# Feed-forward input with stationary weights, and rstd carried by rows and to the output

## The chip, the core and the metric

The kernel runs on one core of one Trainium2 chip. The core has five engines with queues of their own: TensorE (PE in the profile, its weight loads PEld), VectorE (DVE), ScalarE (ACT), GpSimd (POOL) and SyncE (SP, which here only starts transfers). TensorE multiplies a stationary operand of 128 x 128, loaded ahead, with a moving operand of up to 512 columns, and writes to PSUM; the other engines work on SBUF, and VectorE and ScalarE on PSUM too. The metric is the time of one execution on the device in microseconds (us).

## The reference: one decoder layer over 256 tokens

One sequence of 256 tokens with 1024 features goes through a mixer of two branches (block attention and a linear recurrence), cross-attention over 256 memory tokens, and a gated feed-forward block, all in float32. The change lies in the last block and the final norm:

```
hn = rmsnorm(h, norm_ffn_g)                 # h * rstd(h) * gain
gu = hn @ w_ffn_in                          # 1024 -> 2 x 2816
h  = h + (silu(gu[..., :2816]) * gu[..., 2816:]) @ w_ffn_out
return rmsnorm(h, final_norm_g)
```

Here rstd is one number for each token, 1 / sqrt(mean of squares + 1e-6).

## The kernel before: three products for one, and weight blocks in order

**Numbers in two parts.** Every float32 operand of the large products is split into a high part, which TensorE's fast 32-bit format holds exactly, and a low part, the rest. A product is then three: high by high, high by low, low by high. Weights arrive as raw float32 and are split in the kernel by `prep`: ScalarE writes the high part (line 193), VectorE and POOL share the low part (line 197). One block is 1 MB (128 x 2048), and a block's products are called a unit here. `ORDER` lists the blocks, `nxt` gives the next one and prepares two ahead; three buffers each hold high and low parts, two hold raw blocks.

**Two forms of product.** `t_part` (lines 237 to 239) keeps tokens stationary: 128 tokens by 128 features are loaded, and 512 columns of weights stream past, three times for the three products. The result has tokens on partitions. `gemm_f` (lines 252 and 253) keeps weights stationary: 128 features by 128 outputs are loaded, and all 256 tokens stream past. Where the weight's high part is stationary, the tokens' high and low parts go through in one matmul of 2 x 256 columns, into two halves of a PSUM bank; for the weight's low part there is a second matmul of 256 columns, the tokens' high part alone, added to the first half. The result has output units on partitions, and the two halves of the bank still have to be summed; `ev_sum` does that. Before, this form is used for the keys and queries of the cross-attention alone (tile `psf`), on M2 (memory tokens, buffer P0) and on H1 (tokens, buffer P1).

**The feed-forward block before.** H, the residual stream, has tokens on partitions. `turn_h2(t, c)` (lines 1061 to 1065) transposes a quarter of it (token half t, feature half c) on TensorE, multiplies with the gain on VectorE, and splits it into h2h on ScalarE and h2l on POOL. rstd is not applied here. Quarters are turned while the product before, `wo_part` into `pso`, still runs; the last quarter, (1, 1), after the first `ffn_in`. The inner 2816 units are worked in eleven rounds of 256. `ffn_in` forms gate and value side by side in a bank of 512 columns for each token half (tile `psi`, 24 matmuls a block, two blocks a round). `gate` applies rstd as a scale per partition, in Silu and in the product. Its result has tokens on partitions, and the output product needs inner units there, so `turn_hid` transposes it with four matmuls on TensorE (tile `hidT`, line 1096) and `split` makes its two parts. `ffn_out` adds the round into four accumulators (tile `acc`, `out_part`), one round behind. At the end `out_part` runs by hand-picked pieces, with the last `turn_hid` after the first of them; then `add_out`, the final norm's sums and the stores.

**What sets the order.** TensorE's instructions stand in the order of the program text. The order on the other engines comes from the framework's scheduler, except in stretches under `manual_schedule`, of which the final norm is one. An engine runs its queue in order, so an instruction that waits holds up what stands behind it. PSUM has eight banks: four in pool `mm` (products) and four in pool `sm` (small work, and `acc` in the end).

Of the kernel before, what the change touches and what calls it, by code (L numbers as in the profile page):

```python
# [71 lines left out]
def lay(ws):  # L72
    out = np.empty((len(ORDER), 128, 2048), np.float32)
    for i, u in enumerate(ORDER):
        if u[0] == "F":
            w = ws[u[1]][:, u[2]:u[2] + 256]
            out[i].reshape(128, 8, 256)[...] = w.reshape(8, 128, 256).transpose(1, 0, 2)
        elif u[0] == "T":
            w = ws[u[1]][u[3] * 512:(u[3] + 1) * 512, u[2]:u[2] + 512]
            if i < 3:  # L80
                n = PIECES[i]
                out[i].reshape(n, 128, 4 // n, 512)[...] = w.reshape(n, 4 // n, 128, 512).transpose(0, 2, 1, 3)
            else:
                out[i].reshape(128, 4, 512)[...] = w.reshape(4, 128, 512).transpose(1, 0, 2)
        elif u[0] == "I":
            o = out[i].reshape(128, 4, 512)
            for m in range(2):
                w = ws["w_ffn_in"][u[2] * 512:(u[2] + 1) * 512, m * FH + u[1] * 256:m * FH + (u[1] + 1) * 256]
                o[:, :, m * 256:(m + 1) * 256] = w.reshape(4, 128, 256).transpose(1, 0, 2)
        else:  # L90
            w = ws["w_ffn_out"][u[1] * 256:(u[1] + 1) * 256]
            out[i].reshape(128, 2, 1024)[...] = w.reshape(2, 128, 1024).transpose(1, 0, 2)
    return out
# [24 lines left out]
def build(tc, A, out):  # L118
    nc = tc.nc
    V, SC, G, PE, SY = nc.vector, nc.scalar, nc.gpsimd, nc.tensor, nc.sync  # L120
    with ExitStack() as ctx:
# [119 lines left out]
        def by_k(w, k):  # L241
            return tuple(t.rearrange("p (k c) -> p k c", k=k) for t in w)

        def gemm_f(X2, evict):
            w = by_k(nxt(), 8)
            for m in range(2):
                a = slice(m * 128, (m + 1) * 128)
                ps = mm.tile([128, 2, 256], F32, name="psf", tag="mm")  # L250
                for k in range(8):
                    PE.matmul(ps, w[0][:, k, a], X2[:, :, k], start=k == 0, stop=False)  # L252
                    PE.matmul(ps[:, 0], w[1][:, k, a], X2[:, 0, k], start=False, stop=k == 7)  # L253
# [708 lines left out]

        def ev_sum(dh, dl, c):
            def ev(m, ps):
                t, u = t2b("kx", (128, 256)), t2("ku", (128, 256))
                SC.activation(u, ps[:, 1], AF.Copy)
                V.tensor_tensor(t, ps[:, 0], u, op=ALU.add)
                d = 2 * c + m
                SC.activation(dh[:, d], t, AF.Copy)
                G.tensor_tensor(dl[:, d], t, dh[:, d].bitcast(F32), op=ALU.subtract)  # L970
            return ev
# [76 lines left out]
        at[0] += 4  # L1048
        gfin = big("B4", "gfin", (128, 1024))
        SY.dma_start(gfin, A["gfin"].to_broadcast([128, 1024]))  # L1050
        h2h = big("B1", "h2h", dt=F32R)
        h2l = big("B2", "h2l", dt=F32R)
        def wo_part(ps, t, c, kh):
            t_part(ps, wo[2 * c + kh], (oxh, oxl), t, kh)

# [21 lines left out]


        ring = ("B7", "B14", "B10", "B11", "B12", "B6")
        X2 = (h2h, h2l)  # L1080
        hid, acc, two, psi, hm = {}, {}, {}, {}, {}

        def gate(o, t):
            r, ps = two["r"][:, t:t + 1], psi.pop((o, t))
            g = t2("fg", (128, 256))
            SC.activation(g, ps[:, 0:256], AF.Silu, scale=r)  # L1086
            u = t2b("fu", (128, 256))
            V.scalar_tensor_tensor(u, ps[:, 256:512], r, g, op0=ALU.mult, op1=ALU.mult)  # L1088
            hm[o, t] = u

        def turn_hid(o):
            bk = mm.tile([128, 2, 256], F32, name="hidT", tag="mm")
            for t in range(2):
                u = hm.pop((o, t))
                for j in range(2):
                    PE.transpose(bk[:, j, t * 128:(t + 1) * 128], u[:, j * 128:(j + 1) * 128], ident)
            hd = big(ring[o % 6], "hid", (128, 2, 2, 256), F32R)
            split(bk, hd[:, 0], hd[:, 1])
            hid[o] = hd

        def ffn_in(o, kh, t, w):
            if kh == 0:
                psi[o, t] = mm.tile([128, 512], F32, name="psi", tag="mm")
            t_part(psi[o, t], w, X2, t, kh)

        def out_part(o, w, t, c, home=None, u=0, v=512):
            if home is None and (t, c) not in acc:
# [52 lines left out]

        def add_out(ps, t, u, w):
            d = H[:, t, u:w]
            V.tensor_tensor(d, ps, d, op=ALU.add)
# [89 lines left out]
```

## Time and profile before

| | |
|---|---|
| time, median of 3 runs (lowest to highest) | 625.71 us (625.56 to 626.14) |
| the profiled execution | 625.74 us |
| its span, first to last instruction | 623.8 us |
| TensorE busy in the span | 615.6 us, 99% |
| VectorE, ScalarE, POOL busy | 62%, 53%, 59% |
| mean granted clock of TensorE | 0.997 of full speed |
| feed-forward block, from the first `psi` matmul | 431.8 us to the end |

The page of the profile gives busy times by engine, the span in 40 slices, the chain of work that ended last, and groups of instructions by source line. The timeline gives single instructions with start and length. A matmul's record runs from its start to the end of its passage through the array, and the next one starts before that; lengths of stretches of TensorE are therefore taken from start to start. In rows of a tile, three numbers of nanoseconds are the shortest, the median and the longest.

### The profile page before, as it was taken

The numbers are of one execution on the slowest core, as the hardware profiler recorded it, in microseconds if no ns is written. First come the engines' busy times: TensorE is split into PE (matmuls) and PEld (weight loads), VectorE is DVE, ScalarE is ACT, GpSimd is POOL, SyncE is SP. The second block draws the span as 40 slices with busy tenths as digits, with TensorE's granted clock in tenths as the row PEclk, the third lists the DMA queues.
The fourth block names the chain that finished last, engine by engine and source line by source line (L and its number), as shares of the span: only waits on it lengthen the run. The fifth ranks groups of instructions, "written<-read, shape, count | busy, mean of one in ns | idle before, by whom it ended". The sixth has DMA issues, their size and how long they took to land.

```text
span 623.8 us, 8477 instructions
## 1 busy us (share of the span) xinstructions
PE 615.6 (99%) x3135; PEld 513.1 (82%) x3135; DVE 386.8 (62%) x671; ACT 332.5 (53%) x537; POOL 371.0 (59%) x296
## 2 busy tenths in 40 slices
PE   8999999999999999999999999999999999999995
PEld 7888888888877877778888889888888888888884
DVE  7566878979766875748856456754444444444433
ACT  7775555234376856727447556644543444434432
POOL 3887834556544464355867876656655665566553
PEclk9999999999999999999999999999999999999998
DMA  8755353344433333545455545453355555455511
GB/s 344 290 210 194 143 189 148 135 136 143 188 143 136 136 136 134 204 169 185 157 211 187 182 174 187 140 199 134 133 179 172 192 203 185 169 190 198 203 68 67
DMA packets 16888, 107.50 MB, mean 172 GB/s; under 512 B 2000, under 2 KB 2640, under 8 KB 4560
## 3 DMA queue, kind: packets, MB, share of 16 engines
q1 hardware_dynamic: 16128, 106.14, 46.6%
q10 hardware_dynamic: 720, 0.84, 0.4%
q8 instruction: 24, 0.39, 0.3%
q14 instruction: 16, 0.13, 0.1%
HBM read 105.92 MB, written 1.05 MB: 171 GB/s over the span
## 4 chain that ended last, share of the span: by engine, by line
PE 98%; DMA 1%; POOL 0%; DVE 0%; issue 0%; ACT 0%; POOLq 0%; DVEq 0%; ACTq 0%
PE pst L237 14%; PE pst L239 14%; PE pst L238 14%; PE psi L237 6%; PE psi L239 6%; PE psi L238 6%; PE psf L252 5%; PE acc L237 3%; PE acc L239 3%; PE acc L238 3%; PE psf L253 2%; PE lp L609 2%; PE psg L511 1%; PE pso L237 1%; PE pso L239 1%; PE pso L238 1%
## 5 line engine op out<-in xcount | busy, mean ns | idle before, releaser
L197 POOL TENSOR_TENSOR lo<-raw,hi 128x448 fp32r<-128x448 f32 x172 | 270.2, 1587 | 182.4 <-ACT hi L193 179.5
L193 ACT ACTIVATE hi<-raw 128x1024 fp32r<-128x1024 f32 (+1 forms) x194 | 196.2, 1037 | 167.4 <-PE pst L239 61.0
L197 DVE TENSOR_TENSOR lo<-raw,hi 128x576 fp32r<-128x576 f32 (+2 forms) x194 | 199.0, 1031 | 134.1 <-ACT hi L193 131.9
L237 PE MATMUL pst<-hi,Xh 128*128 128x512 f32 x256 | 103.2, 403 | 0.0
L239 PE MATMUL pst<-hi,Xl 128*128 128x512 f32 x256 | 100.0, 391 | 0.0
L238 PE MATMUL pst<-lo,Xh 128*128 128x512 f32 x256 | 99.9, 390 | 0.0
L237 PE MATMUL psi<-hi,h2h 128*128 128x512 f32 x176 | 69.7, 396 | 0.0
L239 PE MATMUL psi<-hi,h2l 128*128 128x512 f32 x176 | 68.7, 390 | 0.0
L238 PE MATMUL psi<-lo,h2h 128*128 128x512 f32 x176 | 68.6, 389 | 0.0
L239 PEld LDWEIGHTS pst<-hi,Xl 128*128 128x128 f32 x256 | 48.1, 188 | 10.3
L237 PEld LDWEIGHTS pst<-hi,Xh 128*128 128x128 f32 x256 | 48.1, 188 | 9.8 <-issue 0.7
L238 PEld LDWEIGHTS pst<-lo,Xh 128*128 128x128 f32 x256 | 48.2, 188 | 9.1
L239 PEld LDWEIGHTS psi<-hi,h2l 128*128 128x128 f32 x176 | 33.0, 188 | 7.1
L238 PEld LDWEIGHTS psi<-lo,h2h 128*128 128x128 f32 x176 | 33.1, 188 | 6.6
L237 PEld LDWEIGHTS psi<-hi,h2h 128*128 128x128 f32 x176 | 33.1, 188 | 6.5
L237 PE MATMUL acc<-hi,hid 128*128 128x512 f32 x86 | 33.6, 391 | 0.0
L239 PE MATMUL acc<-hi,hid 128*128 128x512 f32 x86 | 33.5, 390 | 0.0
L238 PE MATMUL acc<-lo,hid 128*128 128x512 f32 x86 | 33.5, 389 | 0.0
L1088 DVE SCALAR_TENSOR_TENSOR fu<-psi,r_h,fg 128x256 f32<-128x256 f32 x22 | 10.6, 484 | 26.0 <-ACT fg L1086 26.0
L1086 ACT ACTIVATE fg<-psi,r_h 128x256 f32<-128x256 f32 x22 | 10.4, 475 | 29.9 <-PE psi L239 29.9
L252 PE MATMUL psf<-H,hi 128*128 128x512 f32 x64 | 22.8, 400 | 0.0
L252 PE MATMUL psf<-M,hi 128*128 128x512 f32 x64 | 22.5, 396 | 0.0
(344 smaller groups left out, 1127.0 us busy)
## 6 DMA issues: line engine op xcount, KB each, us to landing
raw<-w SPq DMA_DIRECT2D x94, 1024.0 KB, 4.8
raw<-w SPq DMA_DIRECT2D x4, 512.0 KB, 6.3
raw<-w SPq DMA_DIRECT2D x4, 256.0 KB, 4.2
H<-xtok SPq DMA_DIRECT2D x1, 1024.0 KB, 9.5
mraw<-mT SPq DMA_DIRECT2D x1, 1024.0 KB, 4.9
xraw<-xT SPq DMA_DIRECT2D x1, 512.0 KB, 6.4
gfin<-gfin SPq DMA_DIRECT2D x1, 512.0 KB, 3.7
out<-H SPq DMA_DIRECT2D x2, 256.0 KB, 2.0
```

What stands on the lines that cost most here:

```text
L193: SC.activation(hi[:, a], raw[:, a], AF.Copy)
L197: eng.tensor_tensor(lo[:, b], raw[:, b], hi[:, b].bitcast(F32), op=ALU.subtract)
L237: PE.matmul(ps, xh, h, start=first, stop=False)
L238: PE.matmul(ps, xh, l, start=False, stop=False)
L239: PE.matmul(ps, xl, h, start=False, stop=last)
L252: PE.matmul(ps, w[0][:, k, a], X2[:, :, k], start=k == 0, stop=False)
L253: PE.matmul(ps[:, 0], w[1][:, k, a], X2[:, 0, k], start=False, stop=k == 7)
L511: PE.matmul(pss[c][t], z[:, k, t * 128:(t + 1) * 128], ws[c][0][:, k], start=z is Xh and k == 0, stop=False)
L609: PE.matmul(ps[:, j], KS[:, a0 + j], QQ[:, a0 + j], start=True, stop=True)
L1086: SC.activation(g, ps[:, 0:256], AF.Silu, scale=r)
L1088: V.scalar_tensor_tensor(u, ps[:, 256:512], r, g, op0=ALU.mult, op1=ALU.mult)
```

## The change

The input product of the feed-forward block takes the form of `gemm_f`. A block now holds all 1024 features of 128 gate and 128 value columns, in place of 512 features of 256 and 256. Each block gives one PSUM bank for the gate (m = 0) and one for the value (m = 1), with inner units on partitions, so `turn_hid` is gone. h2h and h2l become two halves of one tile H2 in buffer P0, so that both parts of all tokens stream in one matmul.

rstd now varies along columns. For the gate, `rows_of` spreads it over all partitions (two transposes and a copy), and VectorE multiplies with these rows ahead of Silu. For the value it is left out, and `add_out` multiplies with it when the accumulated output is added to H, since it is a factor of a whole token there. `halves` sums the two parts of a bank: ScalarE copies the one, VectorE adds the other. The high part of the result is written by ScalarE and the low part by POOL, by VectorE in the last round's second block.

At the start, two blocks are taken together and four banks are held: the first four of eight feature groups for all four banks, `turn_h2(1, 1)` after the first bank's share, then rstd and `rows_of`, then the second four.

```diff
 lay(), blocks "I":
-            o = out[i].reshape(128, 4, 512)
+            o = out[i].reshape(128, 8, 256)
             for m in range(2):
-                w = ws["w_ffn_in"][u[2] * 512:(u[2] + 1) * 512, m * FH + u[1] * 256:m * FH + (u[1] + 1) * 256]
-                o[:, :, m * 256:(m + 1) * 256] = w.reshape(4, 128, 256).transpose(1, 0, 2)
+                c = m * FH + u[1] * 256 + u[2] * 128
+                o[:, :, m * 128:(m + 1) * 128] = ws["w_ffn_in"][:, c:c + 128].reshape(8, 128, 128).transpose(1, 0, 2)
...
+        def f_part(ps, w, X2, m, ks):
+            a = slice(m * 128, (m + 1) * 128)
+            for k in ks:
+                PE.matmul(ps, w[0][:, k, a], X2[:, :, k], start=k == 0, stop=False)
+                PE.matmul(ps[:, 0], w[1][:, k, a], X2[:, 0, k], start=False, stop=k == 7)
+
+        def halves(dst, ps):
+            u = t2("ku", (128, 256))
+            SC.activation(u, ps[:, 1], AF.Copy)
+            V.tensor_tensor(dst, ps[:, 0], u, op=ALU.add)
...
-        h2h = big("B1", "h2h", dt=F32R)
-        h2l = big("B2", "h2l", dt=F32R)
+        H2 = big("P0", "H2", (128, 2, 8, 256), F32R)
+        h2h, h2l = H2[:, 0], H2[:, 1]
...
-        def gate(o, t):
-            r, ps = two["r"][:, t:t + 1], psi.pop((o, t))
-            g = t2("fg", (128, 256))
-            SC.activation(g, ps[:, 0:256], AF.Silu, scale=r)
+        def gate(o, kh, m, ps):
+            if m == 0:
+                g = gates[o, kh] = t2("fg", (128, 256))
+                halves(g, ps)
+                V.tensor_tensor(g, g, rows2, op=ALU.mult)
+                SC.activation(g, g, AF.Silu)
+                return
+            if kh == 0:
+                hid[o] = big(ring[o % 6], "hid", (128, 2, 2, 256), F32R)
+            hh, hl = hid[o][:, 0, kh], hid[o][:, 1, kh]
             u = t2b("fu", (128, 256))
-            V.scalar_tensor_tensor(u, ps[:, 256:512], r, g, op0=ALU.mult, op1=ALU.mult)
-            hm[o, t] = u
-
-        def turn_hid(o):
-            bk = mm.tile([128, 2, 256], F32, name="hidT", tag="mm")
-            for t in range(2):
-                u = hm.pop((o, t))
-                for j in range(2):
-                    PE.transpose(bk[:, j, t * 128:(t + 1) * 128], u[:, j * 128:(j + 1) * 128], ident)
-            hd = big(ring[o % 6], "hid", (128, 2, 2, 256), F32R)
-            split(bk, hd[:, 0], hd[:, 1])
-            hid[o] = hd
-
-        def ffn_in(o, kh, t, w):
-            if kh == 0:
-                psi[o, t] = mm.tile([128, 512], F32, name="psi", tag="mm")
-            t_part(psi[o, t], w, X2, t, kh)
+            halves(u, ps)
+            V.tensor_tensor(u, u, gates.pop((o, kh)), op=ALU.mult)
+            SC.activation(hh, u, AF.Copy)
+            (V if (o, kh) == (NF // 2 - 1, 1) else G).tensor_tensor(hl, u, hh.bitcast(F32), op=ALU.subtract)
...
+        ws = [by_k(nxt(), 8) for _ in range(2)]
+        psi = {(i, m): f_bank("psi") for i in range(2) for m in range(2)}
+        for i in range(2):
+            for m in range(2):
+                f_part(psi[i, m], ws[i], H2, m, range(4))
+                if (i, m) == (0, 0):
+                    turn_h2(1, 1)
+        r_2 = rstd2(ssq2, "h2")
+        rows2 = rows_of(r_2, "h2", "rowsB")
+        for i in range(2):
+            for m in range(2):
+                f_part(psi[i, m], ws[i], H2, m, range(4, 8))
+                gate(0, i, m, psi[i, m])
...
-            w = by_k(nxt(), 4)
-            for t in range(2):
-                ffn_in(o, kh, t, w)
-                if (o, kh, t) == (0, 0, 0):
-                    turn_h2(1, 1)
-                    two["r"] = rstd2(ssq2, "h2")
-                if kh == 1:
-                    gate(o, t)
-            if kh == 0 and o:
-                turn_hid(o - 1)
+            w = by_k(nxt(), 8)
+            for m in range(2):
+                ps = f_bank("psi")
+                f_part(ps, w, H2, m, range(8))
+                gate(o, kh, m, ps)
...
         out_part(n - 1, wa, 0, 0)
-        turn_hid(n)
         out_part(n - 1, wa, 0, 1)
...
         def add_out(ps, t, u, w):
             d = H[:, t, u:w]
-            V.tensor_tensor(d, ps, d, op=ALU.add)
+            V.scalar_tensor_tensor(d, ps, r_2[:, t:t + 1], d, op0=ALU.mult, op1=ALU.add)
```

More of the change, by code (lines that the diff above doesn't have):

```diff
@@ L242, in by_k, with f_bank @@
             return tuple(t.rearrange("p (k c) -> p k c", k=k) for t in w)
+        def f_part(ps, w, X2, m, ks):
[3 more added lines that the diff above has]
+                PE.matmul(ps[:, 0], w[1][:, k, a], X2[:, 0, k], start=False, stop=k == 7)
+        def f_bank(name):
+            return mm.tile([128, 2, 256], F32, name=name, tag="mm")
+        def halves(dst, ps):
+            u = t2("ku", (128, 256))
+            SC.activation(u, ps[:, 1], AF.Copy)
+            V.tensor_tensor(dst, ps[:, 0], u, op=ALU.add)
         def gemm_f(X2, evict):
@@ L248, in gemm_f @@
             for m in range(2):
[L249 to L253, printed above, removed]
+                ps = f_bank("psf")
+                f_part(ps, w, X2, m, range(8))
                 evict(m, ps)
@@ L964, in ev @@
             def ev(m, ps):
-                t, u = t2b("kx", (128, 256)), t2("ku", (128, 256))
-                SC.activation(u, ps[:, 1], AF.Copy)
-                V.tensor_tensor(t, ps[:, 0], u, op=ALU.add)
+                t = t2b("kx", (128, 256))
+                halves(t, ps)
                 d = 2 * c + m
@@ L1079, in build @@
         ring = ("B7", "B14", "B10", "B11", "B12", "B6")
-        X2 = (h2h, h2l)
-        hid, acc, two, psi, hm = {}, {}, {}, {}, {}
-        def gate(o, t):
-            r, ps = two["r"][:, t:t + 1], psi.pop((o, t))
-            g = t2("fg", (128, 256))
-            SC.activation(g, ps[:, 0:256], AF.Silu, scale=r)
-            u = t2b("fu", (128, 256))
-            V.scalar_tensor_tensor(u, ps[:, 256:512], r, g, op0=ALU.mult, op1=ALU.mult)
-            hm[o, t] = u
-        def turn_hid(o):
-            bk = mm.tile([128, 2, 256], F32, name="hidT", tag="mm")
-            for t in range(2):
-                u = hm.pop((o, t))
-                for j in range(2):
-                    PE.transpose(bk[:, j, t * 128:(t + 1) * 128], u[:, j * 128:(j + 1) * 128], ident)
-            hd = big(ring[o % 6], "hid", (128, 2, 2, 256), F32R)
-            split(bk, hd[:, 0], hd[:, 1])
-            hid[o] = hd
-        def ffn_in(o, kh, t, w):
-            if kh == 0:
-                psi[o, t] = mm.tile([128, 512], F32, name="psi", tag="mm")
-            t_part(psi[o, t], w, X2, t, kh)
+        hid, acc, gates = {}, {}, {}
+        def gate(o, kh, m, ps):
[8 more added lines that the diff above has]
+            hh, hl = hid[o][:, 0, kh], hid[o][:, 1, kh]
+            u = t2b("fu", (128, 256))
+            halves(u, ps)
+            V.tensor_tensor(u, u, gates.pop((o, kh)), op=ALU.mult)
+            SC.activation(hh, u, AF.Copy)
+            (V if (o, kh) == (NF // 2 - 1, 1) else G).tensor_tensor(hl, u, hh.bitcast(F32), op=ALU.subtract)
         def out_part(o, w, t, c, home=None, u=0, v=512):
```

## The prediction

> **What bounds the kernel now.** I read the page first (busy times, slices, the chain that ended last), then the waits of TensorE, then the timeline of TensorE unit by unit.
>
> ```profile
> PE 615.6 (99%) x3135; PEld 513.1 (82%) x3135; DVE 386.8 (62%) x671; ACT 332.5 (53%) x537; POOL 371.0 (59%) x296
> PEclk9999999999999999999999999999999999999998
> PE 98%; DMA 1%; POOL 0%; DVE 0%; issue 0%; ACT 0%; POOLq 0%; DVEq 0%; ACTq 0%
> ```
> ```profile
> PE warm L327 <- DVE still L324: 1.6, 1, 1.6
> ```
>
> TensorE is the bound: 98% of the chain is its own, its clock is granted in full, and after the start it has one listed wait, 1.6 us before the first matmul. No other engine is above 62%. So the change is worth what it does to TensorE's stream: the spacing of its matmuls, the transposes it issues, and any new wait. Busy time is no measure of the spacing, because one matmul's record overlaps the next; I use differences of starts.
>
> **The old unit and the turn.** A unit is one 1 MB block of weights. This is the timeline of TensorE (start, length, instruction).
>
> ```profile
> 448.62 0.60 PE L1096 MATMUL hidT<-cst,fu 128*128 128x128 f32 x4
> ...
> 594.37 0.39 PE L237 MATMUL psi<-hi,h2h 128*128 128x512 f32 x1
> ...
> 599.81 0.60 PE L1096 MATMUL hidT<-cst,fu 128*128 128x128 f32 x4
> 600.17 0.48 PE L237 MATMUL psi<-hi,h2h 128*128 128x512 f32 x1
> ...
> 605.74 0.39 PE L237 MATMUL acc<-hi,hid 128*128 128x512 f32 x1
> ```
>
> A feed-forward input unit is 24 matmuls of 512 columns: 599.81 - 594.37 = 5.44 us, 226.7 ns each. From the first turn (448.62) to the tenth (599.81) nine rounds pass, 151.19 us, 16.80 each. A round is two input units, one output unit (the same 24 matmuls) and one turn, so a turn costs 16.80 - 3 x 5.44 = 0.48 us: 0.36 for the four transposes and the rest in a slow restart behind them.
>
> **Removed: eleven turns.** 11 x 0.48 = 5.28 us, all on the path, since nothing else holds TensorE up there. The last one, between two output parts, interrupts the same stream, so I price it alike.
>
> **Changed: 22 input units.** Column counts are equal: old 24 x 512 = 12288, new 16 pairs of 512 and 256 = 12288. But the new unit has 32 matmuls and 32 weight loads, not 24. The kernel already runs this form in cross-attention (`gemm_f`), so its spacing can be read:
>
> ```profile
> 334.12 0.47 PE L252 MATMUL psf<-M,hi 128*128 128x512 f32 x1
> ...
> 350.85 0.39 PE L237 MATMUL pst<-hi,M 128*128 128x512 f32 x1
> ```
> ```profile
> 361.76 0.39 PE L252 MATMUL psf<-H,hi 128*128 128x512 f32 x1
> ...
> 373.05 0.28 PE L237 MATMUL xs<-kxh,qxh 128*128 128x256 f32 x1
> ```
>
> The first stretch is three units on M2, 48 pairs in 16.73 us with one slow restart of 0.09 in it (read below): (16.73 - 0.09) / 48 = 346.7 ns a pair, 5.55 a unit. The second is two units on H1, 32 pairs in 11.29 us: 352.8 ns, 5.645 a unit. So a new unit is dearer than an old one by 0.107 or by 0.205 us, over 22 units 2.35 or 4.51 us. The two stretches differ in the buffer that streams. H2 takes the tag P0, which is the one M2 had; H1 had P1. I therefore take 2.35 and keep 4.51 for the range. This is the weakest choice in the sum: the trace doesn't show that the buffer is the cause.
>
> Below both lies the price by columns alone, 1.5 x 226.7 = 340 ns a pair and no difference. The Trainium skill, "TensorE: Matmul & The Clock Gate", section "Back-to-back issue gap", gives N / 2.4 + 2.5 ns for an isolated stream, which I work out as an estimate of 5.18 us for the old unit and 5.20 for the new; with that the whole change would come to about -3.0 us, near 622.7. The same section says that in a real kernel the weight load counts too, and its rule for a load, columns / 1.2, makes an estimate of 107 ns, as long as the 256-column matmul it hides behind, which speaks against the change; by the two stretches above the trace sides with that second statement.
>
> **Moved: the opening.** Old, the first unit began with tokens 0 to 127 alone. New, its first matmul streams all 256 tokens, high and low parts, so it waits for `turn_h2(1, 0)` to its last step, the subtraction on POOL. The timeline there:
>
> ```profile
> 429.12 2.78 POOL L197 TENSOR_TENSOR lo<-raw,hi 128x448 fp32r<-128x448 f32 x2
> 430.42 0.63 ACT L1064 ACTIVATE h2h<-h2g 128x512 fp32r<-128x512 f32 x1 [1.64 <-DVE h2g L1063]
> 431.81 0.39 PE L237 MATMUL psi<-hi,h2h 128*128 128x512 f32 x1
> 431.86 1.29 POOL L1065 TENSOR_TENSOR h2l<-h2g,h2h 128x512 fp32r<-128x512 f32 x1
> 432.01 0.69 DVE L914 TENSOR_TENSOR H<-pso,H 128x512 f32<-128x512 f32 x1 [1.63 <-PE pso L239]
> 433.99 0.70 POOL L288 TENSOR_TENSOR r_h<-v__4067,nhalf 128x2 f32<-128x2 f32 x1 [0.84 <-DVE v__4067 L286]
> 434.54 0.60 PE L1061 MATMUL h2T<-cst,H 128*128 128x128 f32 x4
> 435.17 0.69 DVE L1063 TENSOR_TENSOR h2g<-h2T,gv 128x512 f32<-128x512 f32 x1 [1.25 <-PE h2T L1061]
> 435.89 0.63 ACT L1064 ACTIVATE h2h<-h2g 128x512 fp32r<-128x512 f32 x1 [2.38 <-DVE h2g L1063]
> 436.60 1.29 POOL L1065 TENSOR_TENSOR h2l<-h2g,h2h 128x512 fp32r<-128x512 f32 x1 [1.91 <-ACT h2h L1064]
> ```
>
> POOL comes to that subtraction only after two weight pieces (429.12 + 2.78 = 431.90) and ends it at 433.15. The built order of POOL, VectorE and ScalarE up to this point is the same in both kernels, so 433.15 stands. How TensorE resumes is seen where it starts after a ScalarE copy:
>
> ```profile
> 4.58 0.63 ACT L193 ACTIVATE hi<-raw 128x512 fp32r<-128x512 f32 x1 [1.92 <-DMA x0g<-x0g]
> ...
> 5.27 0.78 PE L511 MATMUL psg<-hi,Xh 128*128 128x512 f32 x2
> 5.89 0.63 PE L511 MATMUL psg<-hi,Xl 128*128 128x512 f32 x2
> ```
>
> It starts 0.06 after the releaser (5.21 to 5.27), and two matmuls take 0.62 where 2 x 0.227 = 0.45 would do: 0.17 lost. New first start 433.15 + 0.06 = 433.21, against 431.81: 1.40 + 0.17 = 1.57 us. If POOL were free at once after ScalarE (431.05 + 1.29 + 0.06 = 432.40), it would be 0.76; hidden altogether, 0.
>
> What is late next: from 433.21, four pairs and the restart end at 434.77, four transposes at 435.13, and `h2` is whole 436.60 + 1.29 - 434.54 = 3.35 us after these start, 438.1. Twelve more pairs keep TensorE until 439.4. So the second halves are covered by 1.3 us; r_h, ready at 434.69, is earlier still. The third unit's weights are ready before, as now.
>
> **Added: two transposes for `rows_of`.** The kernel has such a pair already, at the same kind of place:
>
> ```profile
> 327.56 0.38 PE L294 MATMUL rb<-cst,r_m 128*128 128x128 f32 x2
> 327.69 0.48 PE L252 MATMUL psf<-M,hi 128*128 128x512 f32 x1
> 328.01 0.28 PE L253 MATMUL psf<-M,lo 128*128 128x256 f32 x1
> ```
>
> 0.13 for the pair, and 0.32 to the next start where the stretch above needs about 0.23: 0.09. Together 0.22 us.
>
> **Added beside the path: the evictions.** Rows of the tiles psf and kxh, the table load, two weight pieces on ScalarE, one round of engine time (busy us of PE, PEld, DVE, ACT, POOL), and the last round's weight pieces on POOL:
>
> ```profile
> L966 ACT ACTIVATE ku<-psf x16: 362/367/406, 330.8 to 388.8; 128x256 f32<-128x256 f32 x16
> L967 DVE TENSOR_TENSOR kx<-psf,ku x16: 411/418/418, 333.4 to 389.6; 128x256 f32<-128x256 f32 x16
> L969 ACT ACTIVATE kxh<-kx x8: 417/418/422, 333.8 to 353.2; 128x256 fp32r<-128x256 f32 x8
> L970 POOL TENSOR_TENSOR kxl<-kx,kxh x8: 730/734/742, 334.3 to 355.4; 128x256 fp32r<-128x256 f32 x8
> L1086 ACT ACT_TABLE_LOAD   x1: 1283/1283/1283, 440.7 to 440.7; - x1
> ```
> ```profile
> 437.99 2.01 ACT L193 ACTIVATE hi<-raw 128x1024 fp32r<-128x1024 f32 x2 [1.46 <-PE psi L239]
> ```
> ```profile
> 465.42:482.22 16.80, 16.80 (x77) 13.90 (x76) 7.68 (x9) 7.35 (x9) 10.08 (x6) 1.00 0.55 189
> ```
> ```profile
> 595.75 3.35 POOL L197 TENSOR_TENSOR lo<-raw,hi 128x448 fp32r<-128x448 f32 x2 [1.77 <-ACT hi L193]
> ```
>
> Per round ScalarE gains four copies (0.37) and two casts (0.42) and loses one 512-wide cast; VectorE gains four sums (0.42) and four products of about that length and loses three operations; POOL gains two subtractions (0.73). That makes some 9, 9.5 and 11.5 us of a 16.7 us round: none is the bound. Four PSUM banks cover the evictions: a bank is wanted again three half-units (8.3 us) after its last matmul, and copy and sum take 0.8, so 7.5 us of standing in line behind weight pieces are covered. POOL's pieces end at 599.10 for a unit that starts at 605.74, 6.6 us of cover against 0.73 more ahead of them. Without the cover each us of lateness would be a us of the span. The tightest place is the opening, where four banks are held at once. The second half of the third unit wants the bank of the first unit's second half, whose copy stands in ScalarE behind two weight pieces, the table load and a Silu. Going on from 439.4 with the 0.22 above and 8 + 8 + 8 pairs, it is wanted at 447.9. The pieces can start when the first unit's matmuls end, 442.4, and then 2.01 + 1.28 + 0.4 (Silu, like a cast) + 0.37 + 0.42 and five hand-overs of 0.06 free it at 447.2, 0.7 us early. I cost that at nothing.
>
> At the end the old turn gave way to copy, sum, product, cast, subtraction on ScalarE and VectorE, about 2.1 us, while TensorE has three output parts of six matmuls (4.1 us) to do: nothing. `add_out` on the last piece becomes the three-operand form:
>
> ```profile
> L1207 DVE SCALAR_TENSOR_TENSOR H<-H,r_f,gfin 128x256 f32<-128x256 f32 x2 | 0.9, 480 | 0.7 <-POOL r_f L1174 0.7
> L1163 DVE TENSOR_TENSOR H<-end,H 128x256 f32<-128x256 f32 x2 | 0.8, 424 | 0.3 <-PE end L239 0.3
> ```
>
> 480 against 424 ns, once on the tail: 0.06. The weights keep their bytes and their order on SP's queue: nothing.
>
> **Sum.** -5.28 + 2.35 + 1.57 + 0.22 + 0.06 = -1.08 us. The profiled execution took 625.74 us, 0.03 above the median of 625.71, so I forecast 624.7.
>
> **Rivals.**
> - The pace of H1 (slower than before): 352.8 ns a pair instead of 346.7. Everything else alike: -1.08 + 2.16 = +1.08, 626.8. It decides from where 352 pairs cost the 3.43 us that the other terms save: 340.0 + 9.7, about 349.7 ns. For it: H1 is the later stretch, with loaded engines beside it as here. Against: the buffer is M2's.
> - Columns alone: 340 ns a pair, 5.28 - 1.85 = 3.43 us saved, 622.3. Against it are both stretches. It is the case beside which the page's isolated formula stands.
> - The opening isn't on the path: another order lets POOL finish in time, 1.57 us less to pay, 623.1. For it: only POOL's two pieces and one step after ScalarE make the wait. Against: the built order.
> - A late eviction: the bank in the opening isn't free (0.7 us of margin), or a gate stands behind a weight piece in a round. Priced at 1 to 3 us, 626 to 628. For it: ScalarE's copy now waits in line behind Silu, which waits for VectorE. Against: the same form never held TensorE in cross-attention.
>
> **How the numbers follow.** 0.2% is 1.25 us, about what a measurement of this kernel can tell from no change: below 624.46 is faster, above 626.96 slower. Forecast 0.47, of which 0.16 falls below 624.46 (its own range 624.0 to 625.5) and the rest within. Pace of H1 0.20, half within, half slower. Columns alone 0.09 and no opening wait 0.08, both faster. Late eviction 0.16, a quarter within, the rest slower. Faster 0.33, same 0.45, slower 0.22. The range 623.1 to 627.9 leaves out columns alone and the upper half of the last case, together 0.17.
>
> **What would show it.** Right: in the timeline after, no `hidT`; input units 5.55 us apart by first start; one TensorE wait on the POOL subtraction of `H2` with 1.4 us, and no other. Wrong: units at 5.64 or at 5.44; a TensorE wait on VectorE's sums or on weight pieces; a wait of TensorE before the second halves of the opening. The prediction fails most easily on the pair's spacing, since 352 pairs multiply each ns of it to 0.35 us.

## The result, and the profile after

The changed kernel takes 627.32 us (median; 626.97 to 629.62) where the kernel before, run beside it, takes 626.14 (625.56 to 626.61). The ratio is 1.0028, 95% interval 1.0020 to 1.0036: the change makes the kernel slower, by 1.3 to 2.3 us. The two medians alone lie 1.2 us apart, and the two traces below 1.6. Forecast were 624.7 us and a range of 623.1 to 627.9.

The profiled execution of the changed kernel took 627.75 us, with a span of 626.0 against 623.8 before. These are its busy times, the chain that ended last, and TensorE's waits:

```profile
PE 616.6 (99%) x3269; PEld 518.3 (83%) x3269; DVE 426.7 (68%) x727; ACT 348.4 (56%) x593; POOL 388.7 (62%) x317
PE 97%; POOL 2%; DVE 0%; issue 0%; ACT 0%; POOLq 0%; DVEq 0%
PE warm L339 <- DVE still L336: 1.6, 1, 1.6
PE psi L249 <- POOL H L1077: 1.2, 1, 1.2
```

TensorE is still the bound, and there is one new wait, the one on POOL that the forecast held. So what the forecast missed must lie in how closely matmuls follow each other. The timeline of TensorE shows it (start, length, instruction). First come cross-attention's first matmul, then the feed-forward layer from one output unit (`acc`) to the next input units (`psi`), then the last output units:

```profile
328.29 0.48 PE L249 MATMUL psf<-M,hi 128*128 128x512 f32 x1
...
457.07 0.40 PE L237 MATMUL acc<-hi,hid 128*128 128x512 f32 x1
...
462.58 0.39 PE L249 MATMUL psi<-H,hi 128*128 128x512 f32 x1
...
473.87 0.40 PE L237 MATMUL acc<-hi,hid 128*128 128x512 f32 x1
...
608.22 0.40 PE L237 MATMUL acc<-hi,hid 128*128 128x512 f32 x1
```

- The first matmul of cross-attention starts at 328.29, before it was 327.69. That 0.60 us lies ahead of everything the change touches, so the change itself is worth 2.2 - 0.6 = 1.6 us in this pair of traces.
- Two input units take 473.87 - 462.58 = 11.29 us: 5.645 each, 352.8 ns a pair. That is the pace of H1, not that of M2.
- From 457.07 to 608.22 nine rounds pass: 151.15 us, 16.79 each. Nine rounds before took 151.19. **The rounds have not become shorter at all.** The turn that is gone (0.48) came back as 2 x 0.205 in the input units and 0.064 in the output unit, which now takes 16.79 - 11.29 = 5.504 us instead of 5.44.

The opening, POOL's rows first and then TensorE's:

```profile
429.66 2.78 POOL L197 TENSOR_TENSOR lo<-raw,hi 128x448 fp32r<-128x448 f32 x2
432.40 1.27 POOL L1077 TENSOR_TENSOR H<-h2g,H 128x512 fp32r<-128x512 f32 x1
```
```profile
432.12 0.39 PE L239 MATMUL pso<-hix,ox 128*128 128x512 f32 x1
433.72 0.50 PE L249 MATMUL psi<-H,hi 128*128 128x512 f32 x1 [1.20 <-POOL H L1077]
...
435.23 0.60 PE L1073 MATMUL h2T<-cst,H 128*128 128x128 f32 x4
```

POOL takes up the subtraction of `H2` only behind its two weight pieces and ends it at 433.67; TensorE starts 0.05 later. Without the wait it would have gone on at 432.12 + 0.23 = 432.35, so 1.37 us are lost, and the first four pairs take 435.23 - 433.72 = 1.51 where 4 x 0.353 = 1.41 would do: 1.47 in all.

With the measured sizes, and the turns and the tail as forecast, the sum closes: -5.28 (turns) + 22 x 0.205 = 4.51 (input units) + 11 x 0.064 = 0.70 (output units) + 1.47 (opening) + 0.22 (`rows_of`) + 0.06 (tail) = +1.68, against the 1.6 of the traces. All but the opening leaves +0.21: what the turns gave, the spacing took back.

### The profile page after: what moved, and what is told of

It is laid out like the page before. It is cut to its first block, busy times and chain, and to the rows that moved or that the text cites. A ratio compares the mean times of both kernels' runs of the same rounds, so it can differ in the third digit from the quotient of the medians.

```text
span 626.0 us, 8908 instructions
## 1 busy us (share of the span) xinstructions
PE 616.6 (99%) x3269; PEld 518.3 (83%) x3269; DVE 426.7 (68%) x727; ACT 348.4 (56%) x593; POOL 388.7 (62%) x317
## 4 chain that ended last, share of the span: by engine, by line
PE 97%; POOL 2%; DVE 0%; issue 0%; ACT 0%; POOLq 0%; DVEq 0%
PE pst L237 14%; PE pst L239 14%; PE pst L238 14%; PE psi L249 13%; PE psi L250 7%; PE psf L249 5%; PE acc L237 3%; PE acc L239 3%; PE acc L238 3%; PE psf L250 2%; PE lp L621 2%; PE psg L523 1%; PE as L770 1%; PE ao L803 1%; PE aT L794 1%; POOL lo L197 1%
## 5 line engine op out<-in xcount | busy, mean ns | idle before, releaser
L197 POOL TENSOR_TENSOR lo<-raw,hi 128x448 fp32r<-128x448 f32 x172 | 265.3, 1559 | 168.9 <-ACT hi L193 165.9
L197 DVE TENSOR_TENSOR lo<-raw,hi 128x576 fp32r<-128x576 f32 (+2 forms) x194 | 208.8, 1082 | 111.7 <-ACT hi L193 110.4
L249 PE MATMUL psi<-H,hi 128*128 128x512 f32 x352 | 125.0, 399 | 1.2 <-POOL H L1077 1.2
L250 PE MATMUL psi<-H,lo 128*128 128x256 f32 x352 | 98.8, 281 | 0.0
L249 PEld LDWEIGHTS psi<-H,hi 128*128 128x128 f32 x352 | 66.1, 188 | 17.8 <-POOL H L1077 1.6
L250 PEld LDWEIGHTS psi<-H,lo 128*128 128x128 f32 x352 | 66.5, 189 | 0.3
L1099 ACT ACTIVATE fg<-fg 128x256 f32<-128x256 f32 x22 | 9.2, 419 | 34.3 <-DVE fg L1098 34.2
L1108 POOL TENSOR_TENSOR hid<-fu,hid 128x256 fp32r<-128x256 f32 x21 | 26.3, 1252 | 0.0
L258 ACT ACTIVATE ku<-psi 128x256 f32<-128x256 f32 x44 | 16.2, 371 | 7.8 <-PE psi L250 7.8
L1107 ACT ACTIVATE hid<-fu 128x256 fp32r<-128x256 f32 x22 | 9.2, 419 | 18.4 <-DVE fu L1106 18.4
```

The source lines that it names most:

```text
L197: eng.tensor_tensor(lo[:, b], raw[:, b], hi[:, b].bitcast(F32), op=ALU.subtract)
L1099: SC.activation(g, g, AF.Silu)
L1107: SC.activation(hh, u, AF.Copy)
L1108: (V if (o, kh) == (NF // 2 - 1, 1) else G).tensor_tensor(hl, u, hh.bitcast(F32), op=ALU.subtract)
```

## The experiments

Theory at the start: the spacing of the mixed form (512 and 256 columns in turn) is what the change lost by, and the buffer it streams from doesn't decide it. Rivals: the buffer, the values, the alternation itself, and the opening as the larger loss. Each kernel is the changed kernel with the edit shown; the kernel before ran on the same chip beside it. A whole time without a ratio is that of one execution; there the reading rests on the timeline.

### Does the buffer or the data set the pace?

```
-            gemm_f(H1, ev_sum(qxh, qxl, c))
+            gemm_f(M2, ev_sum(qxh, qxl, c))
```

> The changed kernel, but the four query units of cross-attention stream the memory tokens M2 instead of H1 (so the queries are wrong); all else as it is. It asks whether the pace of a pair, 346.7 ns on M2 and 352.8 on H1, belongs to what is streamed or to the place in the program. If to the operand (its buffer or its values): the 32 pairs of the first two query units take 32 x 346.7 = 11.09 us. If to the place (what runs beside, the state in which TensorE arrives): 32 x 352.8 = 11.29 us as before. The feed-forward units stay at 5.645 us either way.

```
-        ox = big("P1", "ox", (128, 2, 8, 256), F32R)
+        ox = big("P0", "ox", (128, 2, 8, 256), F32R)
...
-        H2 = big("P0", "H2", (128, 2, 8, 256), F32R)
+        H2 = big("P1", "H2", (128, 2, 8, 256), F32R)
```

> The changed kernel with H2 in buffer P1 and the attention output ox in P0, the two exchanged. In the changed kernel H2 streams from the very buffer from which M2 ran at 346.7 ns a pair, and runs at 352.8, so I expect the buffer to be without effect: feed-forward units of 5.645 us, pairs of 352.8 ns. If the address matters in some other way, the pair's time moves by 2 ns or more.

```
+        nogain = cp.tile([128, 4], F32, name="nogain")
+        V.memset(nogain, 0.0)
...
-            V.tensor_tensor(g, bk, bc(gv[:, V_FFN + 4 * c:V_FFN + 4 * c + 4], 128, 2), op=ALU.mult)
+            V.tensor_tensor(g, bk, bc(nogain, 128, 2), op=ALU.mult)
```

> The changed kernel with a gain of zero in the feed-forward norm, so that H2 is all zeros with the same instructions (the feed-forward block then adds nothing). It asks whether the values that stream set the pace. If they do: pairs go to 346.7 ns, units to 5.55 us, and the span is about 2 us shorter. If not: 352.8 ns, 5.645 us, and the same span within 0.4 us.

Two units' first matmul and the first one behind them, in the timeline of TensorE: the query stage on M2, the feed-forward units with H2 in P1, and those with tokens of zeros.

```profile
362.64 0.39 PE L249 MATMUL psf<-M,hi 128*128 128x512 f32 x1
...
373.93 0.28 PE L237 MATMUL xs<-kxh,qxh 128*128 128x256 f32 x1
```
```profile
461.95 0.39 PE L249 MATMUL psi<-H,hi 128*128 128x512 f32 x1
...
473.24 0.40 PE L237 MATMUL acc<-hi,hid 128*128 128x512 f32 x1
```
```profile
462.10 0.39 PE L249 MATMUL psi<-H,hi 128*128 128x512 f32 x1
...
473.39 0.40 PE L237 MATMUL acc<-hi,hid 128*128 128x512 f32 x1
```

All three differences are 11.29 us (whole times 628.02, 627.11 and 627.25). M2 itself runs at 352.8 ns a pair where the queries are computed; the other buffer and zeros change nothing. The buffer, on which the forecast's term rested, is excluded, and so are the values.

### Is it the alternation?

```
             for k in ks:
                 PE.matmul(ps, w[0][:, k, a], X2[:, :, k], start=k == 0, stop=False)
+            for k in ks:
                 PE.matmul(ps[:, 0], w[1][:, k, a], X2[:, 0, k], start=False, stop=k == 7)
```

> The changed kernel, with the 512-column matmuls of a bank issued first and then its 256-column ones, instead of in turn. The trace of before has runs of 512 columns at 226.7 ns and runs of 256 columns at 120 ns (scores, 12 in 1.44 us). Theory that the alternation of lengths makes the slow pace: a unit takes 16 x 226.7 + 16 x 120 = 5.55 us instead of 5.645, 22 units save 2.1 us, the query units another 0.3, and output units behind them return towards 5.44 us, 0.6 us more at most. Theory that the stage sets the pace whatever the order: units stay at 5.645 us and the time is that of the changed kernel within 0.4 us.

```profile
462.03 1.98 PE L249 MATMUL psi<-H,hi 128*128 128x512 f32 x8
...
473.18 0.40 PE L237 MATMUL acc<-hi,hid 128*128 128x512 f32 x1
...
478.64 1.98 PE L249 MATMUL psi<-H,hi 128*128 128x512 f32 x8
```

With one change from short to long a bank, two units take 11.15 us (5.573 each) and the output unit 5.46: 0.07 and 0.04 less. But the whole time rose to 630.25 us, ratio 1.0065 (1.0048 to 1.0081). The new order of matmuls led the scheduler to another order on ScalarE and VectorE: both weight pieces of a block went ahead of the evictions, and these fell behind by some 0.4 us a round. TensorE goes on from a round's first bank to the second at 464.80 in the round that starts at 462.03, and at 597.70 in the last. ScalarE's copies of these two first banks begin 0.2 and 4.1 us later:

```profile
465.00 0.39 ACT L259 ACTIVATE ku<-psi 128x256 f32<-128x256 f32 x1 [0.15 <-PE psi L251]
...
601.76 0.36 ACT L259 ACTIVATE ku<-psi 128x256 f32<-128x256 f32 x1
```

At the end TensorE waited. The wait, and TensorE's timeline around it:

```profile
PE acc L237 <- ACT hid L1108: 2.1, 1, 2.1
```
```profile
611.10 0.50 PE L239 MATMUL acc<-hi,hid 128*128 128x512 f32 x1
613.70 0.55 PE L237 MATMUL acc<-hi,hid 128*128 128x512 f32 x1 [2.10 <-ACT hid L1108]
614.04 0.63 PE L238 MATMUL acc<-lo,hid 128*128 128x512 f32 x1
614.47 0.63 PE L239 MATMUL acc<-hi,hid 128*128 128x512 f32 x1
...
617.03 0.59 PE L239 MATMUL acc<-hi,hid 128*128 128x512 f32 x1
617.45 0.40 PE L237 MATMUL acc<-hi,hid 128*128 128x512 f32 x1
```

The gap from 611.10 to 613.70 cost 2.4 us, and behind it matmuls follow each other in 0.43 us, half pace, until 617.45: eight in 3.41 us, 1.6 more than at 0.227. So the spacing got better as expected, and the whole kernel got worse by a cause that the expectation did not hold. This is the late eviction that the forecast had as a rival; it came with another order of the same work.

### What is the opening worth?

```
-            G.tensor_tensor(h2l[:, ks, ts], g, h2h[:, ks, ts].bitcast(F32), op=ALU.subtract)
+            (V if (t, c) == (1, 0) else G).tensor_tensor(h2l[:, ks, ts], g, h2h[:, ks, ts].bitcast(F32),
+                                                         op=ALU.subtract)
```

> The changed kernel with one subtraction moved from POOL to VectorE: the low part of the third quarter of H2, behind which TensorE waited 1.2 us (listed) and restarted about 0.1 us late. Theory (the opening wait is the POOL queue, 1.47 us on the path): the TensorE wait on POOL goes, TensorE's first matmul on H2 starts about 1.3 us earlier, and the whole time is about 1.3 us under the changed kernel's, close to the kernel before (626.0 where the kernel before has 626.1). Rival (the opening only moves the wait, another engine is as late): less than 0.4 us gained. The units keep 5.645 us.

The whole time is 626.95 us, ratio to the kernel before 1.0006 (0.9997 to 1.0015), not to be told from it. From the first matmul of cross-attention to the end the trace takes 297.1 us, where the changed kernel's takes 297.7. TensorE's wait, VectorE's rows and POOL's beside them:

```profile
PE psi L249 <- DVE H L1077: 0.6, 1, 0.6
```
```profile
430.37 0.68 DVE L1075 TENSOR_TENSOR h2g<-h2T,gv 128x512 f32<-128x512 f32 x1
431.75 1.37 DVE L1077 TENSOR_TENSOR H<-h2g,H 128x512 fp32r<-128x512 f32 x1 [0.70 <-ACT H L1076]
```
```profile
429.79 2.78 POOL L197 TENSOR_TENSOR lo<-raw,hi 128x448 fp32r<-128x448 f32 x2
```

Half of the wait stayed, 0.6 us. VectorE takes 1.37 us for the subtraction, twice the 0.68 of the product just before, though both have 512 columns: the product reads one operand from PSUM, the subtraction both from SBUF, while POOL works on its pieces until 432.57. The Trainium skill, "SBUF — State Buffer", section "Who interferes with whom", says that a VectorE instruction with two SBUF inputs contends with a GpSimd instruction that reads SBUF; these rows agree. So do VectorE's weight pieces of 576 columns in the same trace, both operands in SBUF: 0.77 us where one begins 0.12 ahead of POOL's work, 1.44 beside it. The 0.69 us by which the subtraction is longer account for what is missing from my 1.3; that contention is the reason is read from these rows, no run takes POOL's work away. The opening as the larger loss is excluded by its size, 1.47 us against 4.51 + 0.70 of spacing in the sum; this run alone doesn't show it.

### Is the pace a state that TensorE keeps?

The two stretches of the kernel before differ in a thing the forecast had not weighed: the fast one (three key units) starts behind eight transposes, the slow one (two query units) behind a unit of 512-column matmuls. The next kernel takes that unit away from between them:

```
-    order += tgroup("wkv_x", 1024)[:2]
     order += [("F", "wq_x", c * 256) for c in range(4)]
-    order += tgroup("wkv_x", 1024)[2:]
+    order += tgroup("wkv_x", 1024)
...
-            gemm_f(H1, ev_sum(qxh, qxl, c))
+            gemm_f(M2, ev_sum(qxh, qxl, c))
```

> The changed kernel with the order of cross-attention's units turned: the four query units stand straight behind the four key units, with no 512-column token unit between them, and stream M2 instead of H1 (so the queries, and the output, are not the reference's). Theory A (a stretch keeps the pace with which TensorE entered it, and the 512-column unit between them set the slow one): the first two query units run at the key units' 346 to 347 ns a pair, 5.55 us each. Theory B (the pace belongs to the instructions of the query stage itself): 352.8 ns, 5.645 us. In both the whole time is within 1 us of the changed kernel's.

```profile
335.19 0.47 PE L248 MATMUL psf<-M,hi 128*128 128x512 f32 x1
...
363.01 0.28 PE L236 MATMUL xs<-kxh,qxh 128*128 128x256 f32 x1
```

Between these rows lie five units without a break, three of the keys and two of the queries: 27.82 us, less the 0.09 of a restart and over 80 pairs, 346.6 ns. The query units, slow with M2 behind the 512-column unit, are fast without it. That is theory A: a stretch keeps the pace at which it was entered. The whole time, 628.86, missed the expected 1 us. It is 1.1 us above the changed kernel's profiled execution: 0.5 lies ahead of the first matmul of cross-attention, and 0.7 in the attention's output product (`pso`), whose first 36 matmuls take 8.92 us instead of 8.19, with a listed wait on VectorE among them.

```
+            if kh == 0 and o > 1:
+                dummy = f_bank("dummy")
+                for j in range(8):
+                    PE.transpose(dummy[:, j // 4, 128 * (j % 2):128 * (j % 2) + 128],
+                                 H[:, j // 4, 128 * (j % 4):128 * (j % 4) + 128], ident)
```

> The changed kernel with eight transposes, whose results nobody reads, ahead of the first input unit of nine of the eleven rounds, as there are eight transposes ahead of the key units that ran in 346 to 347 ns a pair. Theory A (the pace is set at entry, and transposes at entry give the fast one): the input units behind them take 5.55 us instead of 5.645, and the two together 11.10 and a restart of 0.09 instead of 11.29. Theory B (entry doesn't matter): 11.29 and the restart. The transposes themselves cost some 0.85 us a round, so the whole time rises by about 7.7 us less what the pace gives back (up to 1.7).

The first three of the nine rounds with transposes, from the first matmul of the input units to that of the output unit:

```profile
463.16 0.48 PE L249 MATMUL psi<-H,hi 128*128 128x512 f32 x1
...
474.54 0.40 PE L237 MATMUL acc<-hi,hid 128*128 128x512 f32 x1
...
480.85 0.48 PE L249 MATMUL psi<-H,hi 128*128 128x512 f32 x1
...
492.23 0.40 PE L237 MATMUL acc<-hi,hid 128*128 128x512 f32 x1
...
498.53 0.48 PE L249 MATMUL psi<-H,hi 128*128 128x512 f32 x1
...
509.71 0.39 PE L237 MATMUL acc<-hi,hid 128*128 128x512 f32 x1
```

11.38, 11.38 and 11.18 us, and so on in threes: less the restart, 352.8, 352.8 and 346.6 ns a pair. The same instructions on the same data run at either pace, and a restart can change it, but not each time. Neither theory as written holds; the state is shown, what picks it is not. The whole time is 634.87 us, 7.5 above the changed kernel's. With two transposes instead of eight (`range(2)`):

> The changed kernel with two transposes, whose results nobody reads, ahead of the first input unit of nine rounds, as there are two ahead of the first key unit, which ran in 346.7 ns a pair. Theory (a restart behind transposes draws the pace anew, sometimes the fast one, as three of nine rounds did behind eight transposes): the two input units take 11.18 us in some rounds and 11.38 in the others, the restart of 0.09 in both. Rival (the number of transposes picks the pace): all nine 11.18, or all nine 11.38.

```profile
462.40 0.48 PE L249 MATMUL psi<-H,hi 128*128 128x512 f32 x1
...
473.79 0.40 PE L237 MATMUL acc<-hi,hid 128*128 128x512 f32 x1
```

All nine rounds took 11.38 to 11.39 us, slow, as the rival had it (whole time 629.29). But the first key unit, also behind two transposes, is fast in every kernel here whose key units alternate. So the number of transposes alone can't be what decides. The trace of before holds a slow unit behind transposes too, the fourth query unit, behind four of them:

```profile
381.94 0.48 PE L252 MATMUL psf<-H,hi 128*128 128x512 f32 x1
...
387.67 0.28 PE L237 MATMUL xs<-kxh,qxh 128*128 128x256 f32 x1
```

5.73 us, less the restart 5.64: 352 ns a pair, in the kernel from which the forecast took its pace. The last kernel of this question enters alternation from a run of short matmuls, in the first bank of a round only:

```
+            if runs:
+                for k in ks:
+                    PE.matmul(ps, w[0][:, k, a], X2[:, :, k], start=k == 0, stop=False)
+                for k in ks:
+                    PE.matmul(ps[:, 0], w[1][:, k, a], X2[:, 0, k], start=False, stop=k == 7)
+                return
...
-                f_part(ps, w, H2, m, range(8))
+                f_part(ps, w, H2, m, range(8), kh == 0 and m == 0)
```

> The changed kernel with the order changed in one bank of four: the first bank of a round's first input unit takes its eight 512-column matmuls first and then its eight 256-column ones; the other three banks alternate. So alternation is entered from a run of short matmuls instead of from the long ones of the output unit. Theory A (the way in sets the pace): the three banks run at 346.7 ns a pair, and two units take 2.79 + 3 x 2.77 = 11.11 us instead of 11.29. Theory B (behind an uninterrupted stream alternation always falls into the slow pace): 2.79 + 3 x 2.82 = 11.25 us.

```profile
462.97 1.98 PE L250 MATMUL psi<-H,hi 128*128 128x512 f32 x8
...
474.21 0.40 PE L237 MATMUL acc<-hi,hid 128*128 128x512 f32 x1
```

11.24 us, as theory B had it: within an uninterrupted stream the three alternating banks are slow again (whole time 627.41).

### Can the terms be mended, and do they add up?

The kernel with all three terms mended takes the order of the fourth kernel and the subtraction of the fifth, and writes the order of ScalarE, VectorE and POOL in the feed-forward loop out by hand:

```
+        with tc.manual_schedule(engines={EN.Activation, EN.DVE, EN.Pool}):
...
+                step(g)
                 ps = f_bank("psi")
...
+                f_part(ps, w, H2, 0, range(8))
+                g_sum(o, kh, ps)
+                step(g)
+                step(g)
+                g_silu(o, kh)
+                ps = f_bank("psi")
+                f_part(ps, w, H2, 1, range(8))
+                g_hid(o, kh, ps)
```

Here `step(g)` issues the next piece of a weight block (`prep` now stops behind each piece), and `g_sum`, `g_silu`, `g_hid` are the parts of `gate`.

> The changed kernel with that subtraction on VectorE, with all 512-column matmuls of a bank ahead of all its 256-column ones, and with the order of ScalarE, VectorE and POOL in the feed-forward loop written out by hand (first weight piece, copy, sum and product of the first half, second weight piece, Silu, then the second half), so that the last block's weight pieces can't get ahead of the evictions. Theory (the loss of the change is the sum of the spacing, 22 units of 0.20 us, the slower output units and the opening wait): input units 5.573 us, output units 5.467, no listed TensorE wait after the first, and 1.6 + 0.36 + 1.3 = 3.2 us under the changed kernel, 624.1, which is 0.3% under the kernel before. Rival (something at the end or in the opening replaces them): 626 or more, with a TensorE wait to be listed.

It takes 624.90 us, ratio to the kernel before 0.9977 (0.9966 to 0.9987): faster than both. Units and output units are as in the fourth kernel, and no wait is left at the end. The profiled execution took 627.2 us, and its extra time lies in its first microseconds on TensorE:

```profile
5.83 1.22 PE L526 MATMUL psg<-hi,Xh 128*128 128x512 f32 x2 [0.70 <-ACT hi L193]
...
9.41 1.05 PE L531 MATMUL psg<-lo,Xh 128*128 128x512 f32 x2
...
10.91 0.63 PE L526 MATMUL psg<-hi,Xl 128*128 128x512 f32 x2
```

From start to start two matmuls take 0.85 us until about 10 us, and 0.47 from 10.91 on: this execution began at half pace (the granted clock on record reads 1.00 even there). In the changed kernel's trace the half pace ends at 6.95. From its first matmul of cross-attention (330.36) to the end it needs 295.0 us; the changed kernel needs 626.0 - 328.29 = 297.7, the kernel before 623.8 - 327.69 = 296.1. So 2.7 of the expected 3.2 us are there, and the 0.5 that is missing is about the half of the opening wait that stayed (0.6).

A smaller edit serves as well: two long matmuls and two short ones in turn.

```
-            for k in ks:
-                PE.matmul(ps, w[0][:, k, a], X2[:, :, k], start=k == 0, stop=False)
-                PE.matmul(ps[:, 0], w[1][:, k, a], X2[:, 0, k], start=False, stop=k == 7)
+            for q in range(ks.start, ks.stop, 2):
+                for k in (q, q + 1):
+                    PE.matmul(ps, w[0][:, k, a], X2[:, :, k], start=k == 0, stop=False)
+                for k in (q, q + 1):
+                    PE.matmul(ps[:, 0], w[1][:, k, a], X2[:, 0, k], start=False, stop=k == 7)
```

> The changed kernel with the 512- and 256-column matmuls of a bank in the order two long, two short, so that TensorE changes from short to long four times a bank instead of eight (alternation) or once (all long ones first). Floor: 16 pairs of 346.7 ns, 5.547 us a unit. Theory A (every change from short to long has a price of its own, the 13 ns that the order with one change a bank showed: 5.573 - 5.547 = 26 ns for two): 8 changes a unit make 5.547 + 0.10 = 5.65 us, no better than alternation. Theory B (the price belongs to the state in which alternation runs, 98 ns a unit in the slow one and none in the fast): between 5.55 and 5.60 us.

```profile
461.29 0.61 PE L250 MATMUL psi<-H,hi 128*128 128x512 f32 x2
...
472.42 0.40 PE L237 MATMUL acc<-hi,hid 128*128 128x512 f32 x1
...
477.87 0.62 PE L250 MATMUL psi<-H,hi 128*128 128x512 f32 x2
```

Two units take 11.13 us (5.57 each), the output unit 5.45, with four times as many changes from short to long as in the fourth kernel. So a change has no fixed price: theory B. ScalarE and VectorE kept their order, no wait came at the end, and the time is 624.69. With the subtraction of the fifth kernel added, it gives the lowest time of all:

> The changed kernel with two edits: the order two long, two short in every bank, and the subtraction of the third quarter of H2 on VectorE. Theory (the loss of the change is spacing, slower output units and the opening, and these two edits act on them independently): input units 5.568 us instead of 5.645 (22 x 0.077 = 1.7), output units 5.450 instead of 5.503 (0.5 over ten), the opening wait 0.6 instead of 1.2 (0.6), so 2.8 us under the changed kernel's 627.3: 624.5, which is 0.25% under the kernel before, with no late evictions at the end. Rival (the two-and-two order's single look was a lucky opening, and the end becomes late as in the order with one change a bank): 626 or more.

```profile
455.99 0.40 PE L237 MATMUL acc<-hi,hid 128*128 128x512 f32 x1
...
605.27 0.40 PE L237 MATMUL acc<-hi,hid 128*128 128x512 f32 x1
```

Nine rounds take 149.28 us, 16.59 each, 0.21 less than before and after. The time is 624.57 us, ratio to the kernel before 0.9978 (0.9969 to 0.9987): 0.22% under it, where 0.25% was expected.

## Why the prediction was wrong

**The step that failed** is the price of the 22 input units: "The two stretches differ in the buffer that streams. H2 takes the tag P0 ... I therefore take 2.35 and keep 4.51 for the range." The measured term is 4.51. The buffer has no part in it (M2 is slow in the query stage, H2 in P1 is as fast as in P0). The two stretches differ in how they were entered, and from the second round on the new units are entered like the slow one, straight out of a stream of 512-column matmuls. The timeline of before showed what stood ahead of each stretch, and a slow unit behind transposes as well. This term alone turns -1.08 into +1.08, the rival "pace of H1". The time lies inside the range only because the range kept 4.51; the direction was wrong.

**A term was missing.** An output unit behind the mixed form takes 5.504 us instead of 5.44, and that makes 0.70 over the kernel. The forecast took units that weren't edited at their old price. Behind the two-and-two order they take 5.45, so it is the form ahead that slows them. With this term the +1.08 becomes +1.78, and the opening's 0.10 less makes the +1.68 of the sum.

**What was right.** The opening: one TensorE wait on POOL's subtraction, 1.47 us where 1.57 was forecast. Its 0.17 for the restart was read at 5.27 us, in the first microseconds, where other traces still run at half pace; the restart here cost 0.10. `rows_of`: 0.13 and 0.09, as forecast. The second halves of the opening, the bank with 0.7 us of margin and the end show no TensorE wait, so the costs put at nothing were nothing. The turns: no `hidT` is left, and the sum closes with the forecast's 5.28.

**What was mis-sized beside the path.** A subtraction of `hid` on POOL takes 1.25 us in the changed kernel, not the 0.73 taken from `kxl`. It cost nothing here. Nor does the estimate of 107 ns for a weight load stand in any row: the loads of `psf` before have records of 187 to 189 ns, and 32 of them would make 6.0 us in a unit of 5.6, so they overlap and give no price. The row of the subtraction:

```profile
L1108 POOL TENSOR_TENSOR hid<-fu,hid 128x256 fp32r<-128x256 f32 x21 | 26.3, 1252 | 0.0
```

**What stays open.** Why a restart behind transposes gives the fast pace sometimes: every third round behind eight transposes, none of nine behind two, never at the fourth query unit behind four, and each time at the first key unit behind two. No run here tells what TensorE's state consists of.

## What to carry to other kernels

When the price of a new form is read from an older stretch, look at what stands on the engine just ahead of that stretch and ahead of the new place; the buffer and the data were the wrong things to compare. Behind a break either pace can come, so price both. Price the neighbours too, since a form that is not edited can run slower behind one that is. When a count of matmuls is multiplied by hundreds, try the order in which sizes alternate: here two long, two short gained 0.077 us a unit over one and one, and with the subtraction moved to VectorE it turned a loss of 0.28% into a gain of 0.22%.

## What the runs showed of the hardware that was not expected

- The same 32 pairs run at 346.6 or at 352.8 ns, the same within a nanosecond in the mean of each whole stretch; zeros instead of data and another buffer left the slow pace as it was. 346.7 is the sum of a steady 512-column matmul (226.7) and a 256-column one in a run (120), so the fast pace has no loss in alternation at all.
- In the fourth kernel a gap of 2.6 us between two starts, behind three spacings of 0.33 to 0.47 us, halved TensorE's pace for 3.41 us (granted clock 0.50, and 1.00 ahead of it and behind). The Trainium skill, "TensorE: Matmul & The Clock Gate", section "What's actually happening", names a window of about 3.4 us that runs freely, an idle one to halve the clock and a busy one to free it. The length of the slow stretch agrees with it; the gap that sufficed here was shorter.
- Two executions can differ by 2 us in their first 11 us alone: the thirteenth matmul of `psg` starts at 10.91 us in the trace of the kernel with all terms mended and at 8.81 in the changed kernel's, and the text of the two is the same up to there. Two single profiles are compared from a common instruction behind it, not from the span.
